# The output projection of a Hymba layer as seven block products, with the sums of its left operands made one product ahead

## The chip, the cores and the metric

The kernel runs on one core of a Trainium2 chip. The metric is the device time of one execution in microseconds (us); each version is run three times or more and the median is taken. The tensor engine is called PE (its weight loads PEld), the vector engine DVE, the scalar engine ACT, GpSimd POOL, and SP is the engine that issues most of the transfers.

## The reference, cut to what matters

One decoder layer is computed for a prompt of 1024 tokens (with 16 meta tokens ahead of it, which are dropped at the end) and for 64 sample tokens (8 sequences of 8). The 16 heads of 128 channels are 6 mLSTM heads (A0 to A5), 6 gated delta rule heads (B0 to B5) and 4 HGRN2 heads (C0 to C3).

```python
D_MODEL = 2048; SEQ = 1024; DEC_BATCH = 8; DEC_SEQ = 8; HEAD_DIM = 128; N_META = 16
MIX = 2048            # 16 heads x 128

# each layer:
#   x += W_out( headRMSNorm(concat[mLSTM heads, gated-DeltaNet heads, HGRN2 heads]) * g * silu(z) )
# all q/k/v/gate columns and the gate z come from one combined projection of RMSNorm(x)
# after the layer:
def _rmsnorm(x, w):
    xf = x.astype(jnp.float32)
    y = xf * lax.rsqrt(jnp.mean(xf * xf, axis=-1, keepdims=True) + EPS)
    return (y * w.astype(jnp.float32)).astype(x.dtype)
```

The output projection, which the change is about, multiplies y (1088 tokens x 2048 channels) by `w_out` (2048 x 2048), in float32. The outputs are the normed sums for the prompt and the sample tokens, and the heads' states.

## The kernel before, in words

**Halves.** The prompt is processed in two halves of 512 tokens; the first also has the 64 sample and the 16 meta tokens (592 columns, `halves[0]`, `half.first`). Each half runs the input projection head by head in the order of `ORDER` (C0 B0 A0 B1 A1 C1 B2 A2 B3 A3 C2 B4 A4 B5 A5 C3), and the scan of each head runs in between.

**Float32 by three products.** The matmuls take float32 operands rounded to a shorter form (`F32R`). So every float32 operand is split in a rounded part (hi, a cast on ACT) and the remainder (lo, a subtraction on DVE), and a product is hi x hi + lo x hi + hi x lo: three matmuls. For weights `feed_split` does this, for y `finish` does. The weights come as pieces of 128 x 512: `pieces` lists them in the order of use, `feed_raw` loads them (256 KB on ACT's queue into `wraw`, 5 buffers) up to 7 ahead, `feed_split` makes `whi` and `wlo` (4 buffers each) up to 3 ahead, and `next_piece` hands out the next.

**The weave.** Scans, finishes and other side work are Python generators in the queues of `Weave` ("scan", "fin", "post", "bg"). Between matmuls, `weave.pump` issues the next step of each queue whose due time has been reached, on a clock that `Clock` and `Engine.cost` keep by estimated costs while the program is written. `drain` and `drain_queue` issue the remaining steps of streams or of a queue, with `pump` alone and no matmul of the projections in between: they push the clock forward to the next due time until those streams are done. Behind that, a scheduler that keeps to the dependencies can still move instructions on each engine, so the order on the engines differs somewhat from the order in the code. All recorded operations carry line 137, the helper's; so groups are told apart by tile names.

**The scans near the change.** The last head is C3. Its scan works in levels: POOL makes X from the exponentials Ex and hk or hq, PE multiplies X into pa, and after the last level hkd and hqd (POOL) feed pkh, puh and poh on PE. After each scan, `finish` normalises the head's output, turns it through DRAM (`turn_out`, `turn_in`: `yd` stores and `s` loads), multiplies it by the gate, splits it (ACT casts into `zs`, POOL subtracts, `y<-y,zs`) and stores both parts in `y_dram`. `load_y` brings them back into the tiles of the projection's input. All transfers other than weight pieces are on SP's queue, in order.

**The output stage.** For each column group `cg` (512 columns) all 16 heads k run over the token tiles of a half: 5 tiles in the first half (the sample tile has 2 products, since both of its y parts lie in one left operand), 4 in the second. Each head's piece is used once per unit. After a unit the sums in PSUM (`oacc`) are added to x (`res`, DVE), squared with a sum along the row (`oscr`, ACT) and multiplied by the final norm's weight (`fnw`, POOL); when all four column groups of a half are done, `final_norm` makes the factor `fr` (a `pow` on POOL), scales and stores. The last column group of the second half is run as two units of two tiles.

Of the kernel before, what the change touches and what calls it, by code (L numbers as in the profile page):

```python
# [13 lines left out]
P = 128  # L14
D = 2048
# [130 lines left out]
class Weave:  # L146
    def __init__(self, clock):
        self.clock = clock
        self.queues = {"scan": [], "fin": [], "post": [], "bg": []}
# [37 lines left out]
OUT_UNITS = ([(cg, range(5)) for cg in range(4)], [(cg, range(4)) for cg in range(3)] + [(3, range(2)), (3, range(2, 4))])  # L187
# [3 lines left out]
def hybrid_step(ctx, tc, i, o):  # L191
# [51 lines left out]
    def o_raw(k, cg):  # L243
        raw = wp.tile([P, 512], F32, tag="wraw", name="wraw", bufs=5)
        WDMA(raw, i["w_out"][0, P * k:P * (k + 1), 512 * cg:512 * (cg + 1)])
        return raw

# [95 lines left out]
    for units in OUT_UNITS:  # L343
        for cg, _ in units:
            for k in range(NK):
                pieces.append((o_raw, k, cg))
# [256 lines left out]
    y_dram = [dp.tile([NH, P, w], F32R, name=f"y{w}") for w in (2 * NSAMP + 2 * HALF, 2 * HALF)]  # L603
# [233 lines left out]

    def finish(half, head, outs, ssq, scale, zs):
# [36 lines left out]
        d = y_dram[half.index][head].bitcast(F32)  # L875
        for part, t in enumerate((yhi, ylo)):
            t = t.bitcast(F32)
            at_ = 2 * NSAMP if half.first else 0
            DMA(d[:, at_ + HALF * part:at_ + HALF * (part + 1)], t[:, 0:HALF])
            if half.first:  # L880
                DMA(d[:, NSAMP * part:NSAMP * (part + 1)], t[:, HALF:WS])
# [90 lines left out]
    def mlstm_scan(half, h, kT, qT, vT, tho, zs, nm, em, st):  # L972
# [118 lines left out]
        weave.add("fin", finish(half, h, hxs, ssq, 0.25, zs))  # L1091
# [60 lines left out]
    def gdn_scan(half, h, ck_, cq, cv, zs, Gb, eG, bb, st):  # L1152
# [242 lines left out]
        weave.add("fin", finish(half, HA + h, hxs, ssq, 1.0, zs))  # L1395
# [22 lines left out]
    def hgrn_scan(half, h, kT, lf, qT, vT, zs, st):  # L1418
# [152 lines left out]
        weave.add("fin", finish(half, HA + HB + h, hxs, ssq, 0.25, zs))  # L1571
# [91 lines left out]
    def load_y(half, g):  # L1663
        w = y_dram[half.index].shape[-1]
        yT[half.index][g] = [hp.tile([P, 2, w], F32R, tag=f"h{g}{part}", name=f"y{g}{part}") for part in (0, 1)]
        for q in range(4):
            DMA(yT[half.index][g][q // 2][:, q % 2].bitcast(F32), y_dram[half.index][4 * g + q].bitcast(F32))

    def y_block(half, k, n, part):

        at_ = HALF * part + P * n
        return yT[half.index][k // 4][k % 4 // 2][:, k % 2, at_:at_ + P]

    hB, yT = {}, [{}, {}]
    for half, groups in zip(halves, group_lists):
# [4 lines left out]
        for n, group in enumerate(groups):  # L1680
# [5 lines left out]
            if half.first and n == 6:  # L1686
                weave.add("bg", prep_B())
            after = None
            if n == len(groups) - 1:
# [3 lines left out]
                else:  # L1693
                    after = lambda g: load_y(halves[0], g)
# [12 lines left out]

    ys_flat = o["y_sample"].rearrange("b t d -> (b t) d")
    tags = ["a", "b", "c", "d", "e", "f", "g", "h", "j", "a", "b", "c", "d", "e", "f", "g", "h", "j", "k", "u"]

    def final_norm(toks, some, res, ss, fr, late):
        for n in some:
            cnt = toks[n][1]
            V.tensor_reduce(fr[:cnt, n:n + 1], ss[:cnt, n], op=ALU.add, axis=AX.X)
            V.tensor_scalar(fr[:cnt, 8 + n:9 + n], fr[:cnt, n:n + 1], 1.0 / D, EPS, op0=ALU.mult, op1=ALU.add)
            G.tensor_tensor(fr[:cnt, 16 + n:17 + n], fr[:cnt, 8 + n:9 + n], halfneg[:cnt, 0:1], op=ALU.pow)
        yield
        for n in some:
            _, cnt, _, dst = toks[n]
            for cg in range(4):  # L1720
                t, r = res[n, cg], fr[:cnt, 16 + n:17 + n]
                if cg == 3 and late:
                    V.scalar_tensor_tensor(t[:cnt], t[:cnt], r, fnw[cg][:cnt], op0=ALU.mult, op1=ALU.mult)
# [112 lines left out]
```

## Time and profile before

| | |
|---|---|
| median of 3 runs | 2504.53 us (2497.64, 2504.53, 2504.58) |
| the profiled execution's own time | 2499.9 us |
| its span, from the first to the last instruction | 2498.2 us |
| mean granted clock of PE | 0.991 |
| busy: PE, PEld, DVE, ACT, POOL | 2437.1, 2181.1, 1441.9, 993.4, 548.7 us |
| moved by DMA | 350.81 MB, 140 GB/s over the span |
| output matmuls, written into `oacc` | 1088 with `whi`, 576 with `wlo` |
| weight pieces: `w_in`, `w_out` | 564 and 144 loads of 256 KB |
| POOL: `res<-res,fnw`, `y<-y,zs` | 34 of 1460 ns, 32 of 1441 ns |
| output stage, first to last output matmul | 2097.5 to 2487.1 us |

The table is read from the page and the windows of the profiled execution; the other rows are shown where they are used. A row of a group gives its line (always 137 here), engine, operation, tiles (out<-in), shape and count, then busy us and the mean ns of one, then how long the engine was idle just before them and what ended that.

### The profile page before, as it was taken

What the parts mean: (1) busy time and instruction counts of PE and PEld (TensorE: products, weight loads), DVE (VectorE), ACT (ScalarE), POOL (GpSimd) and SP (SyncE); (2) the same over time, 40 slices, a digit from 0 to 9 for tenths busy, and PEclk for the clock granted to TensorE, in tenths of its full rate; (3) what the DMA queues carried; (4) which work ended last, traced back from release to release, by engine and by line L of the source; (5) the groups of instructions that cost most, each with busy time, mean ns of one, the idle gap of its engine ahead of it and who ended that gap; (6) DMA issues with size and microseconds to landing.
All of it is one profiled execution on the core that took longest, in us unless ns stands there. A gap on an engine that the chain in (4) does not pass through costs nothing.

```text
span 2498.2 us, 43685 instructions
## 1 busy us (share of the span) xinstructions
PE 2437.1 (98%) x16032; PEld 2181.1 (87%) x16032; DVE 1441.9 (58%) x3080; ACT 993.4 (40%) x2428; POOL 548.7 (22%) x743
## 2 busy tenths in 40 slices
PE   6999999999999999999999999999999999999998
PEld 5999999999999999998787888888888888888886
DVE  7765766766647656556854556554654646333435
ACT  5643444443435334343642343343533334222324
POOL 5331211421204212113320113110310102111201
PEclk9999999999999999999999999999999999999999
DMA  6445756766645445348445445454544559526735
GB/s 138 111 119 144 175 131 135 187 147 159 147 108 142 99 119 146 93 112 244 112 121 123 112 120 135 118 134 98 144 118 112 132 124 307 135 84 201 252 100 181
DMA packets 681043, 350.81 MB, mean 140 GB/s; under 512 B 260004, under 2 KB 622076, under 8 KB 680828
## 3 DMA queue, kind: packets, MB, share of 16 engines
q10 hardware_dynamic: 318528, 185.64, 29.4%
q1 hardware_dynamic: 362300, 162.37, 24.9%
q8 instruction: 126, 2.06, 0.3%
q14 instruction: 89, 0.73, 0.1%
HBM read 285.71 MB, written 62.19 MB: 139 GB/s over the span
## 4 chain that ended last, share of the span: by engine, by line
PE 77%; DVE 8%; DMA 6%; issue 3%; ACT 2%; POOL 2%; SPq 1%; ACTq 0%; DVEq 0%; POOLq 0%
PE acc L137 53%; PE oacc L137 13%; DVE wlo L137 2%; DMA wraw<-in_w_in_dram 2%; PE pa L137 1%; PE po L137 1%; SPq L1209 1%; PE pyy L137 1%; PE nd L137 1%; DMA Bb<-db 1%; ACT whi L137 1%; PE pu L137 1%; PE pz L137 1%; DVE Yc L137 1%; DVE Yt L137 1%
## 5 line engine op out<-in xcount | busy, mean ns | idle before, releaser
L137 DVE TENSOR_TENSOR wlo<-wraw,whi 128x512 fp32r<-128x512 f32 x720 | 540.2, 752 | 552.5 <-ACT whi L137 534.7
L137 PE MATMUL acc<-hA,whi 128*128 128x288 f32 (+1 forms) x4544 | 819.6, 302 | 5.3 <-DVE whi L137 5.1
L137 ACT CAST whi<-wraw 128x512 fp32r<-128x512 f32 x720 | 443.9, 618 | 934.9 <-PE acc L137 427.5
L137 PE MATMUL acc<-hB,whi 128*128 128x512 f32 x2272 | 725.3, 401 | 3.6 <-DMA hB<-hblo 3.1
L137 PEld LDWEIGHTS acc<-hA,whi 128*128 128x128 f32 x4544 | 676.1, 190 | 10.2 <-issue 6.5
L137 PE MATMUL acc<-hA,wlo 128*128 128x288 f32 x2240 | 488.5, 298 | 4.7 <-DVE wlo L137 4.7
L137 PEld LDWEIGHTS acc<-hB,whi 128*128 128x128 f32 x2272 | 415.4, 190 | 85.6 <-DMA hB<-hblo 3.9
L137 PE MATMUL acc<-hB,wlo 128*128 128x512 f32 x1120 | 441.6, 394 | 1.5 <-DVE wlo L137 1.5
L137 PEld LDWEIGHTS acc<-hA,wlo 128*128 128x128 f32 x2240 | 365.7, 189 | 6.3 <-DVE wlo L137 6.3
L137 PE MATMUL oacc<-whi,y 128*128 128x512 f32 x1088 | 343.2, 390 | 0.0
L137 PEld LDWEIGHTS acc<-hB,wlo 128*128 128x128 f32 x1120 | 212.1, 189 | 49.4 <-DVE wlo L137 3.4
L137 PEld LDWEIGHTS oacc<-whi,y 128*128 128x128 f32 x1088 | 204.3, 188 | 42.8 <-ACT whi L137 0.8
L137 PE MATMUL oacc<-wlo,y 128*128 128x512 f32 x576 | 224.6, 390 | 2.0 <-DVE wlo L137 2.0
L137 PEld LDWEIGHTS oacc<-wlo,y 128*128 128x128 f32 x576 | 108.2, 188 | 25.4 <-DVE wlo L137 3.3
L137 POOL TENSOR_TENSOR res<-res,fnw 128x512 f32<-128x512 f32 (+1 forms) x34 | 48.6, 1460 | 258.5 <-ACT oscr L137 258.5
L137 POOL TENSOR_TENSOR y<-y,zs 128x592 fp32r<-128x592 f32 (+1 forms) x32 | 46.1, 1441 | 153.2 <-ACT zs L137 138.9
L137 POOL TENSOR_TENSOR qd<-qT,emb 128x512 f32<-128x512 f32 x12 | 16.9, 1404 | 219.1 <-PE po L137 219.0
L137 DVE TENSOR_TENSOR Yt<-Yc,Bb 128x60 f32<-128x60 f32 (+8 forms) x180 | 36.5, 203 | 47.5 <-DMA Bb<-db 42.4
L137 POOL TENSOR_TENSOR hr<-hr,halfneg 128x4 f32<-128x4 f32 (+1 forms) x48 | 44.7, 931 | 70.3 <-DVE hr L137 69.3
L137 POOL TENSOR_TENSOR nrm<-nrm,halfneg 128x10 f32<-128x10 f32 x12 | 24.0, 1998 | 125.0 <-DVE nrm L137 125.0
L137 POOL TENSOR_TENSOR X<-Ex,hk 128x256 f32<-128x256 f32 (+1 forms) x40 | 39.7, 992 | 52.4 <-PE pa L137 40.7
L137 DVE TENSOR_TENSOR Sx<-Sx,lf 128x256 f32<-128x256 f32 (+2 forms) x60 | 35.3, 590 | 20.8 <-ACT Ex L137 18.9
(416 smaller groups left out, 2748.4 us busy)
## 6 DMA issues: line engine op xcount, KB each, us to landing
wraw<-in_w_in_dram ACTq DMA_DIRECT2D x564, 256.0 KB
wraw<-in_w_out_dram ACTq DMA_DIRECT2D x144, 256.0 KB
y<-y SPq DMA_DIRECT2D x16, 576.0 KB
px<-in_x_prompt_dram SPq DMA_DIRECT2D x32, 256.0 KB
yd<-y SPq DMA_DIRECT2D x128, 64.0 KB
out_dram<-sst SPq DMA_DIRECT2D x16, 512.0 KB
s<-yd SPq DMA_DIRECT2D x32, 256.0 KB
y<-zs SPq DMA_DIRECT2D x32, 256.0 KB
```

Source lines behind the costliest of these rows:

```text
L137: return f(out, *a, **k)
L1209: DMA(db[j], Ball[SUB * j:SUB * (j + 1), 0:C, SUB * j:SUB * (j + 1)])
```

## The change

It replaces the two loops over the prompt's tokens in the output stage by Strassen's scheme with seven products, in Winograd's form. The tokens are split in two halves of 512 (rows of A), the heads in `K1` (the first eight of `ORDER`) and `K2` (the last eight), the columns in groups 0, 1 and 2, 3. A11 is then the first half's y of `K1`, A12 that of `K2`, A21 and A22 those of the second half, and B11, B12, B21, B22 the four blocks of `w_out` (B's rows are heads, its columns `cg`). Each product is 512 tokens x 8 heads x 1024 columns, in two column groups j of 8 heads (kk) and 4 tiles with three matmuls. In the order of the code:

| product | left operand | weights | column groups j = 0, 1 |
|---|---|---|---|
| 1 | A11 | B11 | own pieces of `w_out`; sums kept in `t1` |
| 2 | A12 | B21 | own pieces; added to `res` of the first half's cg 0, 1 |
| 3 | A21 - A11 + A22 | T2 | added to `t1` |
| 4 | A21 + A22 | T1 | with `t1` into `q` |
| 5 | A12 minus the left operand of product 3 | B22 | added to `res` of the first half's cg 2, 3 |
| 6 | A11 - A21 | T3 | into `q` and `t1`, which become the second half's `res` |
| 7 | A22 | T4 | added to the second half's cg 0, 1 |

- **Weights.** `combine_weights` is a new generator in a new queue "mix", started with `prep_B` and working after it: 16 pieces, each with 4 loads of 256 KB from `w_out` into `px`/`pxs`, 4 subtractions on POOL, and 4 stores to `w_comb` in DRAM, loads and stores on SP. Products 3, 4, 6 and 7 load their pieces from there (`c_raw`). The pieces loaded in the output stage are 80 of `w_out` and 72 of `w_comb`, against 144 before.
- **Left operands.** `y_whole` holds plain y in DRAM. In the second half `finish` stores only it: the cast into `zs`, the POOL subtraction and the stores of the two parts are gone, and so is `load_y` of the second half. In the first half `finish` stores plain y beside the parts. `fill` runs as a side job of a product: it loads the blocks of y (`yb`) of the next product's left operand, head by head, sums them on POOL (in one place DVE and POOL), and splits the sum into the idle one of the two sets of left operands (`yT[u]`, alternately 0 and 1): 40 casts on ACT and 40 subtractions on DVE in all.
- **Sample tokens** are still multiplied plainly, beside the products (`own` with the product's piece, `other` with a piece of `w_out` loaded for them): 128 matmuls as before.
- **Sums.** `x_rows` and `x_added` load x and add it on POOL; additions of `oacc` to `t1`, `q` and `res` are on DVE. After product 1's first column group the sums are copied on ACT into `px`/`pxs` tiles, and for that "mix" is drained there. The units of the last product, `LAST_UNITS`, are column group 0 with 4 tiles and column group 1 with 2 and 2 tiles.

The diff, cut to its core:

```diff
+HEADS = [{"A": 0, "B": HA, "C": HA + HB}[name[0]] + int(name[1]) for name in ORDER[1:]]
+K1, K2 = HEADS[:NH // 2], HEADS[NH // 2:]
+LAST_UNITS = [(0, range(4)), (1, range(2)), (1, range(2, 4))]
...
+        if not half.first:
+            DMA(y_whole[1][head], y[:, 0:HALF])
+            return
         yhi, ylo = zs.bitcast(F32R), y.bitcast(F32R)
         S.copy(yhi[:, 0:W], y[:, 0:W])
+        ck.last += 1.0
+        yield
+        DMA(y_whole[0][head], y[:, 0:HALF])
+        ck.last = ck.t["T"] + 2.0
...
+    def combine_weights():
+        while not prep_stream.done:
+            yield
+        for j in range(2):
+            for kk in range(NK // 2):
...
+                for t, heads, cg in ((b11, K1, j), (b12, K1, j + 2), (b22, K2, j + 2), (b21, K2, j)):
+                    tc.keep_in_program_order(DMA(t, i["w_out"][0, P * heads[kk]:P * (heads[kk] + 1), 512 * cg:512 * (cg + 1)]))
+                for dst, a, b in ((b11, b12, b11), (b12, b22, b12), (b22, b22, b11), (b21, b21, b22)):
+                    ck.last = ck.t["T"] + 9.0
+                    yield
+                    G.tensor_tensor(dst, a, b, op=ALU.subtract)
+                ck.last = ck.t["T"] + 20.0
+                yield
+                for n, t in (("T1", b11), ("T3", b12), ("T2", b22), ("T4", b21)):
+                    DMA(w_comb[n][NK // 2 * j + kk], t)
...
+    def phase(u, j, accs, tiles, own=None, other=None, each=()):
+        for kk in range(NK // 2):
+            whi, wlo = next_piece()
+            for n in tiles:
+                yh, yl = (y_block(u, kk, n, part) for part in (0, 1))
+                T.matmul(accs[n], yh, whi, start=kk == 0, stop=False)
+                T.matmul(accs[n], yh, wlo, start=False, stop=False)
+                T.matmul(accs[n], yl, whi, start=False, stop=kk == NK // 2 - 1)
+                if n == tiles[0]:
+                    feed_ahead()
+                weave.pump()
...
+            for g in filling:
+                next(g, None)
+            for f in each:
+                f(NK // 2 * j + kk)
...
+    for j in range(2):
+        accs, sacc = banks(), bank("oacc")
+        phase(0, j, accs, halfn, own=(sacc, samples(0)))
+        if j == 0:
+            weave.drain_queue("mix")
+            ck.begin()
+            for n in halfn:
+                t1[j, n] = sp.tile([P, 512], F32, tag="px" if n < 3 else "pxs", name="t1", bufs=3 if n < 3 else 1)
+                S.copy(t1[j, n], accs[n])
+            held = sacc
+    weave.drain_queue("scan")
+    weave.drain_queue("post")
...
+    fill_with(0, [(1, K1), (1, K2), (0, K1)], [(V, 2, ALU.subtract), (G, 1, ALU.add)])
+    for j in range(2):
+        accs, sacc = banks(), bank("oacc")
+        phase(1, j, accs, halfn, own=(sacc, samples(1)), each=[x_rows(1, 0, t1)])
...
+    fill_with(0, [(1, K2)], [])
+    for j in range(2):
+        accs = banks()
+        phase(1, j, accs, halfn, each=[more(1), x_added(q, 5, 2, 2), x_added(t1, 5, 0, 3)])
```

The order of the instructions on PE at the end of C3's scan, early in the output stage, first as it stands before. X_24193 and X_24221 are the operands of the scan's last two levels, y a left operand of the projection; a wait names the engine or transfer it is for.

```order
L137 MATMUL pa<-X_24193 128x128 x3
L137 MATMUL pa<-X_24221 32x32 [waits Pool_49]
L137 MATMUL pa<-Ex 32x64 x2
L137 MATMUL oacc<-whi,y_23848 128x512 [waits DMAHW2_49,Activation_49]
L137 MATMUL oacc<-wlo,y_23848 128x512 [waits DVE_49]
L137 MATMUL oacc<-whi,y_23925 128x512 [waits DMAHW0_49,Activation_49]
L137 MATMUL pkh<-ident,hkd 128x128 [waits Pool_49]
L137 MATMUL puh<-s_24304,s_24342 128x128 [waits DMAHW6_49,Activation_49]
L137 MATMUL oacc<-whi,y_23925 128x512 [waits DMAHW3_49]
L137 MATMUL poh<-state_C_761,hqd 128x128 [waits DVE_49,Pool_49]
```

These are rows out of a stretch of 50; output matmuls without waits lie between all of the steps. The same place after, where the levels' X are X_24415 and X_24425:

```order
L137 MATMUL oacc<-wlo,y_23982 128x512
L137 MATMUL pa<-X_24415 128x128 [waits DVE_49,Pool_49]
L137 MATMUL pa<-X_24415 128x128 x3
L137 MATMUL pa<-X_24425 32x32 [waits Pool_49]
L137 MATMUL pa<-Ex 32x64 x2
L137 MATMUL pkh<-ident,hkd 128x128 [waits DVE_49,Pool_49]
L137 MATMUL pkh<-ident,hkd 128x128 x3
L137 MATMUL puh<-s_24469,s_24477 128x128 [waits DMAHW3_49,Activation_49]
L137 MATMUL poh<-state_C_767,hqd 128x128 [waits Pool_49]
L137 MATMUL poh<-s_24469,AT 128x128 [waits DVE_49]
L137 MATMUL oacc<-whi,y_23853 128x512
```

From the first pa on X_24415 to the first two matmuls of poh, no output matmul is issued; the rows left out only repeat the kinds of matmul shown. POOL at this place, before:

```order
L137 TENSOR_TENSOR X_24221<-Ex,hk 128x8x32 [waits PE_49]
L137 TENSOR_TENSOR X_24221<-Ex,hq 128x8x32
L137 TENSOR_TENSOR hkd<-Sx,hk 128x512 [waits PE_49,Activation_49]
L137 TENSOR_TENSOR hqd<-eP,hq 128x512 [waits PE_49,Activation_49]
L137 COPY state_C_761<-s_24350 128x128 [waits DVE_49,PE_49]
```

And after, where t is a copy of product 1's sums and yb a block of y for a fill:

```order
L137 TENSOR_TENSOR X_24425<-Ex,hq 128x8x32
L137 TENSOR_TENSOR hkd<-Sx,hk 128x512 [waits PE_49,Activation_49]
L137 TENSOR_TENSOR res<-res,t_24532 128x512 [waits DMAHW0_49,Activation_49]
L137 TENSOR_TENSOR res<-res,t_24534 128x512 [waits DMAHW7_49,DVE_49,Activation_49]
L137 TENSOR_TENSOR res<-res,t_24536 128x512 [waits DMAHW1_49,Activation_49]
L137 TENSOR_TENSOR yb<-yb 128x512 [waits DVE_49]
L137 TENSOR_TENSOR hqd<-eP,hq 128x512 [waits PE_49]
L137 TENSOR_TENSOR res<-res,t_24538 128x512 [waits DMAHW2_49,Activation_49,Pool_49]
```

Three additions of x to product 1's sums and one of a fill now stand between hkd and hqd.

More of the change, by code (lines that the diff above doesn't have):

```diff
@@ L1686, in hybrid_step @@
             if half.first and n == 6:
-                weave.add("bg", prep_B())
+                prep_stream = weave.add("bg", prep_B())
+                weave.add("mix", combine_weights())
             after = None
@@ L1729, in final_norm @@
                 yield
+            free.extend(res.pop((n, cg)) for cg in order)
     def norm_states():
@@ new lines, in hybrid_step @@
+    both = sp.tile([P, 2, 512], F32, tag="sst", name="yb", bufs=1)
+    beside = [[both[:, 0], both[:, 1]], [sp.tile([P, 512], F32, tag=f"vx{n}", name="yb", bufs=1) for n in range(2)],
+              [row("a", "yb")[:, 0:512] for _ in range(2)]]
+    ck.begin()
+    for n in halfn:
+        t1[1, n] = free.pop(0)
+        S.copy(t1[1, n], accs[n])
+    for c in range(4):
+        res[0, c] = free.pop(0)
+    for c in range(2):
+        for at_, cg in ((0, c + 2), (NSAMP, c)):
+            DMA(res[0, c + 2][at_:at_ + NSAMP], xs_flat[:, 512 * cg:512 * (cg + 1)])
@@ new lines, in hybrid_step, with more, f @@
+    weave.add("post", sample_done(0, 1))
+    weave.drain_queue("fin")
+    for tag in "ej":
+        free += [row(tag, "res")[:, 0:512] for _ in range(2)]
+    free += [sp.tile([P, 512], F32, tag=f"s{t}", name="res", bufs=1) for t in "56"]
+    def more(x):
+        def f(step):
+            if step == 2:
+                free.extend(beside[x])
+        return f
+    fill_with(1, [(1, K1), (1, K2)], [(G, 1, ALU.add)])
+    for j in range(2):
+        accs, sacc = banks(), bank("oacc")
+        phase(0, j, accs, halfn, other=(sacc, samples(1)), each=[more(2)])
+        ck.begin()
+        for n in halfn:
+            V.tensor_tensor(t1[j, n], t1[j, n], accs[n], op=ALU.add)
+        sample_add(j + 2, sacc)
@@ new lines, in hybrid_step @@
+    weave.drain_queue("post")
+    load_fnw(2)
+    fill_with(0, [(0, K2)], [(G, "hi", ALU.subtract), (G, "lo", ALU.subtract)])
+    for j in range(2):
+        accs, sacc = banks(), bank("oacc")
+        phase(1, j, accs, halfn, other=(sacc, samples(0)))
+        ck.begin()
+        for n in halfn:
+            q[j, n] = free.pop(0)
+            V.tensor_tensor(q[j, n], t1[j, n], accs[n], op=ALU.add)
+        sample_add(j + 2, sacc)
+        weave.add("post", sample_done(j + 2))
+    weave.add("post", final_norm([0], range(4)))
@@ L1801, in hybrid_step @@
+    load_fnw(0)
+    for j, tiles in LAST_UNITS:
+        accs = banks(tiles)
+        phase(0, j, accs, tiles)
+        weave.drain_queue("post")
+        late = tiles[-1] == NC - 1 and j == 1
+        ck.begin()
+        for n in tiles:
+            t = res[n + 5, j] = t1[j, n]
+            V.tensor_tensor(t, t, accs[n], op=ALU.add)
+            squared(n + 5, j, late)
+        if j == 1:
+            weave.add("post", final_norm([n + 5 for n in tiles], (2, 3, 0, 1), late))
     weave.drain_queue("bg")
```

288 lines of the change are left out of this document (195 added, 93 removed).

## The prediction, before the changed kernel was run

> **What bounds the kernel now.** I read the first lines of the page, then the chain of waits over the last 450 us, then a table of windows through the output stage and two of the projection. The page says that one engine is nearly always at work:
>
> ```profile
> span 2498.2 us, 43685 instructions
> ...
> PE 2437.1 (98%) x16032; PEld 2181.1 (87%) x16032; DVE 1441.9 (58%) x3080; ACT 993.4 (40%) x2428; POOL 548.7 (22%) x743
> ```
>
> The chain shows the same from near: early in the output stage (which starts at 2097.5) it runs along PE, and the end of the scan of the last head (C3: pa, pkh, puh, poh) stands between stretches of output matmuls.
>
> ```profile
> 2126.12 0.89 PE pa L137 x8
> 2127.01 9.55 PE oacc L137 x42
> 2136.56 1.71 PE pa L137 x34
> 2138.26 4.53 PE oacc L137 x19
> 2143.24 1.39 PE oacc L137 x6
> 2144.62 0.91 PE puh L137 x8
> 2145.54 1.86 PE oacc L137 x8
> 2147.39 1.78 PE poh L137 x16
> ...
> 2158.26 149.21 PE oacc L137 x658
> ```
>
> The last row gives the price of one output matmul: 149.21 / 658 = 0.2268 us. The windows (start:end, length, then busy time and count of PE, PEld, DVE, ACT, POOL, then clock, DMA share, GB/s) show how little else the stage costs:
>
> ```profile
> 2158.30:2307.50 149.20, 149.20 (x659) 123.54 (x658) 46.56 (x63) 39.76 (x79) 22.35 (x16) 1.00 0.46 139
> 2307.50:2352.00 44.50, 44.27 (x194) 36.04 (x193) 21.58 (x45) 15.02 (x30) 11.43 (x10) 1.00 0.88 296
> 2352.00:2462.60 110.60, 110.60 (x489) 91.55 (x489) 48.05 (x62) 39.00 (x75) 17.00 (x12) 1.00 0.44 125
> 2462.60:2487.10 24.50, 22.75 (x98) 17.94 (x97) 15.06 (x27) 10.33 (x20) 4.25 (x4) 1.00 0.63 201
> 2487.10:2498.20 11.10, 0.62 (x3) 0.19 (x1) 4.87 (x12) 2.85 (x6) 1.54 (x2) 0.76 0.52 189
> ```
>
> PE loses 0.23 us where the halves meet and 1.75 us near the end; then a tail of 11.1 us follows. So a matmul taken out of this stage is time taken out of the span, as long as its feeders keep up.
>
> **What comes off.** Before, the output stage has 64 + 64 pairs of head and column group: 4 groups x 16 heads x (4 tiles x 3 products + 2 of the sample tile) = 896 in the first half and 768 in the second, 1664. After: seven products x 2 column groups x 8 heads x 4 tiles x 3 = 1344, and the sample's 128 as before, 1472. That is 192 fewer: 192 x 0.2268 = 43.5 us off, the gross gain. PE has no other change: the scans and the projection issue what they issued.
>
> **What is added on the path: the drain of the mix queue.** In the order above the drain after the first column group issues all that C3's scan still has, back to back. Before, by the chain, 42 + 19 + 6 + 8 = 75 output matmuls lie between the pa row at 2126.12 and poh: 9.55 + 4.53 + 1.39 + 1.86 = 17.3 us that cover the work of ACT, POOL and DVE between the levels. This cover goes, but those engines do not begin at the drain: X and the exponentials have been issued ahead. What remains behind the drain on POOL is, by the order, X for the last level, hkd, three additions of t onto res, one yb, and then hqd, which the first poh waits for.
>
> ```profile
> L137 POOL TENSOR_TENSOR hkd<-Sx,hk 128x512 f32<-128x512 f32 x1 | 1.5, 1515 | 2.2 <-PE pa L137 2.2
> L137 POOL TENSOR_TENSOR hqd<-eP,hq 128x512 f32<-128x512 f32 x1 | 1.5, 1495 | 2.6 <-PE pa L137 2.6
> L137 POOL TENSOR_TENSOR res<-res,fnw 128x512 f32<-128x512 f32 (+1 forms) x34 | 48.6, 1460 | 258.5 <-ACT oscr L137 258.5
> ```
>
> These are 1.5 + 3 x 1.46 + 1.46 + 1.5 = 8.8 us on POOL from the last level on, while PE has that level's pa (1.71), puh (0.91) and pkh (no longer than puh): 8.8 - 3.5 = 5.3 us of waiting. The lower bound is 2 us (POOL finishes the additions before the level ends, and only ACT's copies of pkh are waited for), the upper the whole cover, 17 us. I take 5.3, since most of the head's X work is hoisted.
>
> A stop of this length can cost clock as well. Two windows in which PE was idle by about as much:
>
> ```profile
> 1160.00:1170.00 10.00, 7.87 (x43) 6.48 (x41) 5.91 (x14) 3.34 (x8) 2.94 (x4) 1.00 0.81 247
> 1170.00:1180.00 10.00, 8.58 (x35) 6.70 (x36) 4.59 (x8) 2.41 (x5) 1.74 (x2) 0.83 1.16 311
> 1320.00:1330.00 10.00, 7.58 (x96) 5.58 (x95) 5.34 (x19) 1.27 (x3) 1.18 (x3) 0.83 0.38 96
> ```
>
> A mean of 0.83 over 10 us is 1.7 us of lost work; I leave it in the bounds, since the first window kept 1.00 with 2.1 us idle. [...]
>
> **What is added beside the path, projection stage.** The weight combinations are 16 pieces of 4 loads (256 KB), 4 POOL subtractions and 4 stores, from 673 us on: 64 x 1.46 = 93 us more on POOL, less 16 x 1.44 = 23 us (the table's mean) of y<-y,zs that the second half no longer does. POOL has room, and so has DMA:
>
> ```profile
> 300.00:650.00 350.00, 347.08 (x2874) 340.46 (x2872) 232.65 (x537) 146.24 (x398) 86.78 (x124) 1.00 0.67 156
> 700.00:1040.00 340.00, 337.62 (x2799) 330.78 (x2798) 205.82 (x485) 135.77 (x375) 82.71 (x118) 1.00 0.48 119
> ...
> 1040.00:1500.00 460.00, 448.20 (x2842) 386.67 (x2841) 270.98 (x593) 189.03 (x440) 93.15 (x108) 0.99 0.52 133
> 1500.00:2053.00 553.00, 551.48 (x3114) 456.68 (x3113) 305.86 (x644) 208.99 (x497) 100.27 (x112) 0.99 0.50 123
> ```
>
> The first window has the nearest thing to the new stream, the preparation of the second half (`prep_B`, which loads x and stores its two parts through SP; DMA share 0.67): PE idle 2.92 of 350 us. The second has none: 2.38 of 340. So such a stream costs about 0.5 us in 350. The new one is four times as long, and its stores wait on POOL with the scans' transfers behind them on SP; the planner also sets the scans by other costs. I take 2.5 us, with bounds from -3 (the second half's finishes lose their cast, subtraction and stores of the parts; the last window has 1.5 us of idle PE to give and the third might give as much) to +12 (the third window, in which the halves meet, has 11.8 us of idle PE: as much again).
>
> **Output stage, beside the path.** Five fills cast 40 blocks on ACT, subtract 40 + 8 on DVE and do 40 operations on POOL; POOL also adds 32 tiles of x or of a product's sum to it, and multiplies 34 by fnw: 106 operations. With rows:
>
> ```profile
> L137 DVE TENSOR_TENSOR wlo<-wraw,whi 128x512 fp32r<-128x512 f32 x142 | 112.8, 799 | 200.0 <-ACT whi L137 192.5 <-DMA wraw<-in_w_out_dram 7.4
> L137 ACT CAST whi<-wraw 128x512 fp32r<-128x512 f32 x141 | 87.4, 621 | 235.8 <-PE oacc L137 173.3 <-DVE wlo L137 20.7 <-DMA wraw<-in_w_out_dram 12.2
> L137 DVE TENSOR_TENSOR res<-res,oacc 128x512 f32<-128x512 f32 (+1 forms) x36 | 23.0, 677 | 10.4 <-PE oacc L137 10.3
> ...
> L137 DVE TENSOR_SCALAR res<-res,fr 128x512 f32<-128x512 f32 (+1 forms) x25 | 13.0, 555 | 5.4 <-POOL fr L137 5.4
> L137 POOL TENSOR_TENSOR fr<-fr,halfneg 128x1 f32<-128x1 f32 (+1 forms) x9 | 7.6, 863 | 21.6 <-DVE fr L137 21.6
> ```
>
> DVE: 152 wlo x 0.80 + 48 x 0.80 + 72 additions x 0.68 + 25 x 0.56 = 223 us. ACT: (152 + 40) x 0.62 = 119, beside as many squares as before. POOL: 106 x 1.46 = 155. PE: 1472 x 0.2268 = 333.8. No engine is near PE on average. The tightest places: the third and fourth products need two pieces per 14 matmuls (3.18 us) where DVE gives 2 x 0.80; the last unit uses one piece per 6 matmuls (1.36 us), as before, and loses what it loses now, the 1.52 us here:
>
> ```profile
> 2470.51 0.50 PE L137 MATMUL oacc<-wlo,y 128*128 128x512 f32 x1 [1.52 <-DVE wlo L137]
> ```
>
> In the sixth product DVE's scalings by fr wait for POOL's pow, with wlo queued behind them; POOL's own queue has the x additions ahead of pow. One POOL operation more in front is 1.46 us, and three pieces stand ready (3 x 12 x 0.2268 = 8.2 us), so I put 2 us on it, from 0 to 8. The last unit now has 8 heads instead of 16: its pieces still come at the same rate, 0.5 us more. The tail has the same operations and stores as now: nothing.
>
> **Sum.** -43.5 + 5.3 + 2.5 + 2 + 0.5 = -33.2 us. Against the profiled execution (2499.9 us, span 2498.2) this is 2466.7. The median of the runs, 2504.53, stands 4.6 us above that execution, the lowest run 2.3 below; I forecast 2468 us for a run like the profiled one, which leaves 1.3 us for that spread.
>
> **Rivals.** (a) The drain loses the whole cover, 17 us, and a clock window, 1.7: 2468 + 11.7 + 1.7 = about 2481. For it: the order leaves one output matmul in the whole stretch. Against it: ACT's and POOL's part of the levels is issued earlier.
>
> (b) DVE becomes the bound of the output stage through POOL. For it: beside POOL's work single wlo take far longer, as here, where POOL's X runs:
>
> ```profile
> 2106.02 1.35 DVE L137 TENSOR_TENSOR wlo<-wraw,whi 128x512 fp32r<-128x512 f32 x1
> ```
>
> From 2158 to 2487 most take half of that (min/median/max in ns):
>
> ```profile
> L137 DVE TENSOR_TENSOR wlo<-wraw,whi x125: 673/693/1843, 2160.6 to 2483.6; 128x512 fp32r<-128x512 f32 x125
> ```
>
> If every POOL operation stops DVE for all its 1.46 us, DVE needs 152 x 0.69 + 48 x 0.69 + 72 x 0.68 + 25 x 0.56 + 155 = 356 us against 334 of PE: 22 us more, 2490. Against it: the mean wlo of the stage is 0.80 and not 0.69 with 34 multiplications on POOL, 142 x 0.11 = 16 us in all and not 34 x 1.46 = 50, and PE lost 1.98 us in the windows above. [...]
>
> (c) The other side: SP is held by the combination's stores. Each piece keeps SP waiting for POOL up to 4 x 1.46 = 5.8 us, 16 pieces 93 us; the scans' transfers queue behind, and heads come late to PE. It decides when more than 33 us of the 93 reach PE beyond the 2.5 of the sum; with half of the 93 the time is 2468 + 46 = 2514. Against it: 1.5 us of idle PE in the 553 us of the last window of the projection, so PE has projection matmuls to do beside scans that come late.
>
> (d) Fewer matmuls without less time, since pieces or y blocks arrive late: the change then only moves the wait to the loads. The window with DMA share 0.88 moved 296 GB/s and cost PE 0.23 us. Of the products after, the third needs up to 16 pieces + 16 blocks of 256 KB (0.262 MB) in the 25.4 us of a column group (112 x 0.2268), 330 GB/s; the sixth some 30 transfers in 21.8 us, 360 GB/s. At 296 GB/s each column group of the third ends 2.9 us late and each of the sixth 4.8, in two and two 15.4 us: 2483. Against it: a fourth of the sixth's are stores, which no matmul waits for. To cancel the change all fourteen column groups would have to be late by 2.4 us.
>
> **Chances.** Forecast 0.65 (its own range 2457 to 2478), (a) 0.12, (d) 0.07, (b) 0.05, (c) 0.07, and 0.04 for an end below 2456, by better covered scans. The range from 2456 to 2489 takes in the forecast, (a) and (d), and leaves out the rest. A difference below 0.3%, 7.5 us, can't be told from none: faster is below 2497, which holds everything but (c): 0.93. (c) has same, 0.02, where little more than a third of its 93 us reaches PE, and slower, 0.05.
>
> **What the next profile would show.** 192 fewer oacc matmuls at 0.227 us. One gap or several short ones on PE, about 5 us, between pa and poh some 25 us into the output stage, with POOL's hqd as the releaser; 17 us would be (a). PE idle in 673 to 2097 as now within some us; if it grows by tens, with SP waiting on POOL, (c). In the output stage a mean wlo near 0.85 us; above 1.2 with PE waiting for wlo throughout, (b). Waits of whi for wraw in the third and fourth products, (d). The forecast is wrong most easily at the drain, and where the order of the scans in the projection stage is moved by the planner's new costs.

## The result, and the profile after

The changed kernel is slower: 2534.23 us in the median of 4 runs (2526.65 to 2546.85) against 2502.68 in the runs of the kernel before that were made beside it; the ratio is 1.0134, with a 95% interval from 1.0088 to 1.0180. The forecast was 2468. The profiled execution took 2537.37 us, its span is 2535.7 us, 37.5 more than before. First the page:

```profile
span 2535.7 us, 44051 instructions
...
PE 2422.4 (96%) x15840; PEld 2160.8 (85%) x15840; DVE 1550.4 (61%) x3168; ACT 1018.6 (40%) x2476; POOL 715.8 (28%) x865
```

192 matmuls are gone, as counted, but PE's busy time fell by 14.7 us only and not by 43.5, and its share fell from 98% to 96%. A table of windows shows where; the first window is the projection, the second the output stage. Before:

```profile
0.00:2097.40 2097.40, 2048.75 (x14267) 1860.42 (x14268) 1272.16 (x2820) 863.34 (x2172) 474.93 (x682) 0.99 0.55 135
2097.40:2487.20 389.80, 387.82 (x1766) 320.54 (x1765) 164.99 (x250) 127.26 (x252) 72.25 (x59) 1.00 0.55 168
```

And after:

```profile
0.00:2132.80 2132.80, 2060.40 (x14266) 1869.22 (x14267) 1298.28 (x2821) 857.27 (x2158) 535.99 (x731) 0.98 0.59 149
2132.80:2524.80 392.00, 361.89 (x1576) 291.62 (x1574) 247.75 (x337) 158.47 (x312) 178.29 (x132) 0.96 0.63 195
```

Both parts failed. The projection, with the same number of matmuls, ends 35.4 us later: PE idles 23.7 us more (72.4 against 48.65) and is busy 11.65 us longer, at a clock of 0.98. The output stage takes 2.2 us more instead of 43.5 less: 28.1 us more idle (30.1 against 2.0), and its 190 fewer matmuls save 25.9 us of busy time instead of 43.5, at a clock of 0.96. The tail is unchanged (10.9 us). What PE waits for in the output stage (us in total, times, longest):

```profile
PE oacc L137 <- ACT whi L137: 14.1, 4, 7.3
PE oacc L137 <- DVE wlo L137: 13.3, 13, 2.5
PE puh L137 <- ACT s L137: 1.6, 1, 1.6
```

So the split weights come late. The longest wait can be followed through the engines' timelines. On SP (L1818 loads x, L1901 a block of y for a fill):

```profile
2387.77 27.36 SPq L1818 DMA_DIRECT2D yb<-in_x_prompt_dram  x9
2415.18 8.08 SPq L1901 DMA_DIRECT2D yb<-yw  x4
```

On ACT, the first cast after that, and the weight cast behind it:

```profile
2419.17 0.62 ACT L137 CAST y<-yb 128x512 fp32r<-128x512 f32 x1 [14.09 <-DMA yb<-yw]
2419.69 0.61 ACT L137 CAST whi<-wraw 128x512 fp32r<-128x512 f32 x1
```

And on PE:

```profile
2420.36 0.79 PE L137 MATMUL oacc<-whi,y 128*128 128x512 f32 x1 [7.34 <-ACT whi L137]
```

Nine loads of x stood on SP for 27 us. The issue of one took 0.33 us in seven of the nine, 0.60 and 0.66 in the other two; for most of the rest SP waited, 12.5 us for POOL's additions, which free the buffers, and 10.0 us for earlier loads of x. The next blocks of y stood behind them on SP, ACT stood 14.1 us for such a block, and the weight cast stood behind that on ACT, although its weights were there (by 2413.4 us). The wait costs more than its length, since the granted clock falls around it:

```profile
2410.00:2420.00 10.00, 3.02 (x9) 2.01 (x7) 0.18 (x1) 0.83 (x2) 7.25 (x6) 0.67 0.42 141
2420.00:2430.00 10.00, 9.62 (x30) 7.35 (x31) 5.57 (x9) 4.87 (x9) 0.00 (x0) 0.70 0.61 192
2430.00:2440.00 10.00, 10.00 (x46) 8.29 (x45) 9.51 (x21) 6.00 (x14) 7.84 (x7) 1.00 0.36 116
```

In the second of these windows PE is busy for 9.62 us and finishes 30 matmuls instead of 42 (9.62 / 0.2268): 2.8 us more than 30 need.

### The profile page after: what moved, and what is told of

It is laid out like the page before. It is cut to its first block, busy times and chain, and to the rows that moved or that the text cites. A ratio compares the mean times of both kernels' runs of the same rounds, so it can differ in the third digit from the quotient of the medians.

```text
span 2535.7 us, 44051 instructions
## 1 busy us (share of the span) xinstructions
PE 2422.4 (96%) x15840; PEld 2160.8 (85%) x15840; DVE 1550.4 (61%) x3168; ACT 1018.6 (40%) x2476; POOL 715.8 (28%) x865
## 4 chain that ended last, share of the span: by engine, by line
PE 62%; DVE 12%; DMA 11%; issue 4%; POOL 4%; ACT 3%; SPq 3%; ACTq 1%; DVEq 0%; POOLq 0%
PE acc L137 47%; PE oacc L137 5%; DVE wlo L137 4%; DMA wraw<-in_w_in_dram 2%; DMA yb<-yw 2%; SPq L1247 2%; DMA Bb<-db 2%; ACT whi L137 1%; PE po L137 1%; PE pyy L137 1%; PE nd L137 1%; DVE Yt L137 1%; POOL yb L137 1%; DVE Yc L137 1%; POOL res L137 1%
## 5 line engine op out<-in xcount | busy, mean ns | idle before, releaser
L137 DVE TENSOR_TENSOR wlo<-wraw,whi 128x512 fp32r<-128x512 f32 x728 | 572.8, 791 | 444.4 <-ACT whi L137 424.8
L137 PE MATMUL oacc<-whi,y 128*128 128x512 f32 x960 | 312.2, 400 | 15.0 <-ACT whi L137 14.1
L137 PEld LDWEIGHTS oacc<-whi,y 128*128 128x128 f32 x960 | 185.5, 193 | 56.3 <-ACT whi L137 16.3
L137 PE MATMUL oacc<-wlo,y 128*128 128x512 f32 x512 | 205.8, 402 | 13.5 <-DVE wlo L137 13.3
L137 PEld LDWEIGHTS oacc<-wlo,y 128*128 128x128 f32 x512 | 98.9, 193 | 41.1 <-DVE wlo L137 20.8
L137 DVE TENSOR_TENSOR y<-yb,y 128x512 fp32r<-128x512 f32 x40 | 36.7, 918 | 47.5 <-ACT y L137 46.7
L137 ACT CAST y<-yb 128x512 fp32r<-128x512 f32 x40 | 24.8, 620 | 82.4 <-POOL yb L137 38.7
L137 POOL TENSOR_TENSOR res<-res,fnw 128x512 f32<-128x512 f32 (+1 forms) x28 | 41.8, 1510 | 42.3 <-ACT oscr L137 42.3
L137 POOL TENSOR_TENSOR yb<-yb 128x512 f32<-128x512 f32 x24 | 34.3, 1432 | 60.3 <-DMA yb<-yw 42.6
```

The costliest lines, as they stand in the source:

```text
L137: return f(out, *a, **k)
```

## The experiments

Two readings serve for all runs: where the projection ends and how long the output stage is, in each run's profiled execution, since the whole time mixes both. Their repeatability follows from kernels that leave one part as it is. With the projection of the changed kernel it ended at 2122.0 to 2137.2 us in eight profiles; with its output stage, that stage took 383.5 to 396.5 in nine. So about 8 us either way can't be told. Ratios are to the kernel before.

### The output stage: the fills

**e1_no_fill**

```diff
     def fill_with(*a):
-        filling.append(fill(*a))
+        pass
```

> All five fills are left out (no blocks of y loaded, summed, cast or split in the output stage), so products 3 to 7 multiply whatever the two sets of left operands held before; matmuls, weight pieces, x rows, squares and stores stay. The output stage took 392.0 us in the changed kernel (2132.8 to 2524.8) where 1472 matmuls at 0.2268 and the scan would be 346. Theory W: the fills' casts on ACT and subtractions on DVE wait for POOL and SP, and weight casts queue behind them: the stage falls to 350-362, PE's waits there from 29.9 us to under 8. Rival L (POOL and DVE lock each other, whoever issues): POOL keeps 66 of its 106 operations, so the stage stays above 372. Rival S (the rest of the side work, x rows and the sample's sums, waits as much): also above 372. Projection as in the changed kernel, 2133 within 8.

```profile
2132.60:2485.70 353.10, 347.07 (x1576) 286.78 (x1574) 196.33 (x289) 138.25 (x272) 123.03 (x92) 0.99 0.55 166
```

353.1 us and 6.0 idle, at 2494.8 us in all (ratio 0.9968, 0.9955 to 0.9982). The forecast for this stage was 389.8 - 43.5 + 5.3 + 2 + 0.5 = 354: without the fills the gain is there, and the fills take 39 us, all of it. The x rows, squares and sums that stay are not the cause by themselves.

**e2_fill_no_wait**

```diff
+                still = yT[1 - u][(kk - 2) // 2][:, (kk - 2) % 2, 2 * NSAMP:2 * NSAMP + HALF].bitcast(F32)
-                S.copy(hi, beside[0][kk % 2])
+                S.copy(hi, still)
...
-                V.tensor_tensor(lo, beside[0][kk % 2], hi, op=ALU.subtract)
+                V.tensor_tensor(lo, still, hi, op=ALU.subtract)
```

> The fills keep every instruction (loads, sums, 40 casts, 40 subtractions), but the casts and subtractions read a block that has long been ready (the hi part of the other set of left operands) instead of the sum; so nothing on ACT or DVE waits for a fill's load or POOL sum, at the same busy time of every engine. Theory W: output stage 392 to 355-370, and waits of PE for whi and wlo from 27 us to under 12. Rival L (the lock, or sheer work): still above 382.

```profile
2131.20:2530.60 399.40, 360.18 (x1576) 292.53 (x1574) 244.74 (x339) 159.50 (x314) 182.22 (x132) 0.95 0.63 195
```

399.4 us, ratio 1.0156 (1.0127 to 1.0186): no gain. But the edit does less than was expected of it. The first fill has eight sums on DVE, and these still wait for its loads, 17.2 us against 4.7 in the changed kernel. And ACT's weight casts now wait for transfers of blocks of y, though they read none:

```profile
DVE yb L137 <- DMA yb<-yw: 17.2, 7, 5.3
ACT whi L137 <- DMA yb<-yw: 15.1, 3, 6.4
ACT whi L137 <- DMA yb<-in_x_prompt_dram: 9.2, 3, 6.2
```

PE's waits for whi and wlo fell from 27.4 to 16.2 us, and the one of 7.3 us is gone. In its place stand two others:

```profile
PE puh L137 <- ACT s L137: 9.5, 1, 9.5
PE oacc L137 <- DVE res L137: 8.7, 2, 7.1
```

The first comes from the DVE sums: DVE's copy of product 1's sample sums stands behind three of them, and ACT's copy s behind that. So e2 neither shows theory W nor refutes it. The loads of the weights are issued on ACT's queue, ahead of the casts, and in the order of e2's program 77 of the stage's 152 wait for one of the eight DMA semaphores that both queues use. That this links the casts to the blocks of y is inferred; no run took it away.

**e5_no_fill_loads, e6_no_fill_sums**: one half of the chain each.

```diff
 # e5
-                    DMA(beside[x][kk % 2], y_whole[half][heads[kk]])
+                    pass
 # e6
-                    e.tensor_tensor(srcs[0], srcs[0], srcs[b], op=op)
-                    ck.sync()
+                ck.sync()
```

> The fills' 72 loads of y blocks are left out (the blocks hold one block loaded once); the sums on POOL and DVE, the casts and the subtractions stay, in their order and with their waits on each other. Theory Q (the transfers: SP's loads wait for buffers that POOL releases late, ACT's casts and the weight loads issued on ACT's queue wait for them, and the 8 DMA semaphores are shared by both queues): the output stage falls from 392 to 354-368. Rival P (the work on POOL and the lock between POOL and DVE): it stays above 380. If both are one chain, this and the next fall.

> The fills' sums (40 operations on POOL, 8 on DVE) are left out; the 72 loads, 40 casts and 40 subtractions stay, so another left operand is multiplied. Rival P: the output stage falls from 392 to 354-368. Theory Q with transfers slow by themselves: above 380. If the loads are slow only because POOL releases their buffers late, it falls here as well as without the loads.

Without the loads, then without the sums:

```profile
2137.20:2497.80 360.60, 349.73 (x1576) 284.94 (x1574) 260.39 (x337) 159.50 (x312) 191.49 (x132) 1.00 0.54 167
```

```profile
2122.00:2492.70 370.70, 354.67 (x1576) 291.10 (x1574) 229.03 (x331) 159.47 (x313) 123.23 (x92) 0.97 0.66 208
```

360.6 and 370.7 of 392.0 (ratios 1.0011, 0.9996 to 1.0025, and 1.0032, 1.0016 to 1.0048): taking away either half brings back 31 and 21 us of the 39. Above the 353.1 us without fills, the sums alone cost 7.5 us and the loads alone 17.6, of which the wait of puh has 5.6 (6.8 us against 1.2); both together cost 39. So the greater part of the loss comes from the two as one chain. e6 ended 3 us above its range. The first row also refutes the lock of rivals L and P, DVE stopped by POOL, as the cause: all of POOL's sums are there, a wlo is as long as in the changed kernel (0.93 us against 0.90), and the stage is 31 us shorter. The wlo groups without loads, without sums:

```profile
L137 DVE TENSOR_TENSOR wlo<-wraw,whi 128x512 fp32r<-128x512 f32 x160 | 146.2, 929 | 72.4 <-ACT whi L137 71.8
```

```profile
L137 DVE TENSOR_TENSOR wlo<-wraw,whi 128x512 fp32r<-128x512 f32 x155 | 126.2, 829 | 89.1 <-ACT whi L137 87.5 <-DMA wraw<-T 1.1
```

With POOL's sums a wlo took 0.10 us longer (0.929 against 0.829, and 0.830 in e1, which has neither), 16 us of DVE in all. PE feels little of it: in e5 it waits 9.1 us for wlo in all, and never more than 1.8.

What SP waits for in the changed kernel's stage shows the chain's other end (L1901 the blocks of y, L1818 x):

```profile
SPq L1901 <- DVE y L137: 87.6, 27, 11.7
SPq L1901 <- POOL yb L137: 46.4, 20, 5.5
```

A block's buffer comes free when POOL has summed it, ACT has cast it and DVE has made the remainder; SP stands until then with the following transfers behind it.

**e9_fill_loads_pool, e12_both**: the loads on another queue; e12 also has the combinations on DVE (e10, below).

```diff
-                    DMA(beside[x][kk % 2], y_whole[half][heads[kk]])
+                    nc.gpsimd.dma_start(beside[x][kk % 2], y_whole[half][heads[kk]])
```

> The fills' 72 loads of y blocks are issued on POOL's queue instead of SP's; nothing else changes. Theory Q (with the loads on SP each waits there for a buffer that POOL, ACT and DVE release one after another, and the x rows and weights wait with them): the output stage falls from 392 to 360-375. Rival: the loads now wait in POOL's own queue, ahead of its sums, and the stage is no shorter than 385.

> Loads of the fills on POOL's queue and combinations on DVE together, everything computed as in the changed kernel. If both help by themselves the two add: projection 2108-2120, output stage 360-375, about 2490; otherwise the sum of the two single results within 8 us.

The stage took 415.1 and 411.6 us, with waits of PE for one weight cast up to 12.9 us; ratios 1.0221 (1.0194 to 1.0249) and 1.0201 (1.0184 to 1.0218). The waiting moved into POOL's own queue, where the loads (L1901) now stand for a buffer, in e9:

```profile
POOL yb L1901 <- DVE y L137: 32.9, 15, 13.9
```

**e14_fill_in_order, e17_deeper**: order and depth.

```diff
 # e14: sums, casts and subtractions of the fills
-                S.copy(hi, beside[0][kk % 2])
+                tc.keep_in_program_order(S.copy(hi, beside[0][kk % 2]))
 # e17: four buffers in products 2 to 4
+    extra = [free.pop(0) for _ in range(4)]
+    deeper += [extra[:2], extra[2:]]
...
+                ahead = len(bufs[x]) - 2
+                for n in (range(ahead + 1) if kk == 0 else [kk + ahead]):
```

> The fills' sums, casts and subtractions may not be moved ahead of anything written before them on their engine. If the order in the queues makes the waits: the output stage falls from 392 to 360-375. If the chain load, sum, cast, subtraction, next load is too long for two buffers whatever the order: 385 or more.

> Everything computed as in the changed kernel, with three edits: the blocks of y of the fills in products 2, 3 and 4 have four buffers instead of two and are loaded two blocks sooner (in product 2 two of the three operands); the first half's finish stores plain y without the shifted steps; the weight combinations' subtractions are on DVE. Projection: 2096.9 without combinations and shifts, some 13 us more with the combinations on DVE, 2105-2115. Output stage: if two buffers were too few, PE's waits in products 3 to 5 go and the stage is 370-380 of 392 (products 6 and 7 keep theirs); if the transfers or the work are slow by themselves, 387 or more. Time 2488-2500 in the first case, 2505-2515 in the second.

390.8 and 392.6 us: neither the order on the engines nor the number of buffers alone changes the stage. In e17 8.4 us of it are the wait of puh (1.6 in the changed kernel), so up to 7 us may be hidden; but PE's waits of over 0.5 us between 100 and 260 us of the stage, where products 3 to 5 lie, still add up to 10.7 us, against 11.5 in the changed kernel. e17 took 2522.67 us (1.0076, 1.0049 to 1.0102), above the time expected, yet the fastest of the kernels that compute everything, through its projection (2107.9). It still has a wait of 7.2 us in product 6, which it did not touch.

**e18_no_added_loads**: the 16 loads of x in product 6, those seen above among them.

```diff
-                pend.append((dst[j, n], x_load(n + n0, j + cg0)))
+                pend.append((dst[j, n], free.pop(0)))
```

> The 16 loads of x in product 6 are left out (POOL adds what the buffers hold); POOL's additions, and the loads of the blocks of y behind them on SP, stay. If SP's order is the cause there: the wait of 7.3 us for a weight cast goes, with its lowered clock, and the output stage is 374-384 instead of 392. If not (the wait comes from POOL's work or ACT's own order): 388 or more.

```profile
PE oacc L137 <- DVE wlo L137: 17.5, 12, 3.0
PE puh L137 <- ACT s L137: 4.2, 1, 4.2
PE oacc L137 <- ACT whi L137: 2.0, 2, 1.1
```

The waits for weight casts fell from 14.1 to 2.0 us and the one of 7.3 is gone: that wait comes from the loads of x on SP. (The edit takes away the loads themselves, not only their place in the queue.) It is no accident of one run: with the same output stage it stands at the same place, 7.5 us long, in e3 and e7. The stage took 384.9 us, 7 less than in the changed kernel, just above the range expected and within the spread; the rest of the loss sits in many waits of 1 to 3 us for wlo.

### The projection: combinations and the finish

**e3_no_mix, e7_mix_no_pool, e8_mix_no_dma**: without the combinations, then with their transfers alone, then with their POOL work alone.

```diff
 # e3; products 3, 4, 6, 7 load plain pieces
-                weave.add("mix", combine_weights())
 # e7
-                    G.tensor_tensor(dst, a, b, op=ALU.subtract)
+                    ck.begin()
 # e8: four tiles loaded once; plain pieces
-                    DMA(w_comb[n][NK // 2 * j + kk], t)
```

> The weight combinations are left out (no loads, POOL subtractions and stores beside the projection); products 3, 4, 6 and 7 load plain pieces of w_out of the same size instead. The projection ended at 2132.8 us against 2097.4 before, 35.4 later: 23.7 of waiting of PE and 11.7 of longer matmuls at a lower clock. Theory M (the mix stream on POOL and SP delays the scans): the projection ends at 2100-2112 and the time falls by 20 us or more. Rival F (the first half's finish, with its extra store and shifted steps, or the order that follows from it): the end stays above 2120; the lag of 6 us at 260 us of the span, ahead of the stream, stays in both.

> The weight combinations' 64 POOL subtractions are left out; the 64 loads and 64 stores stay, so plain blocks of w_out are multiplied. The whole stream cost the projection 23 us (end at 2132.8 with it, 2109.9 without). If POOL's work ahead of the scans' is what costs: the end falls to 2115 or sooner. If SP's queue and DMA: it stays above 2123.

> The weight combinations' loads and stores are left out and their 64 POOL subtractions stay, on four tiles that are loaded once; the products load plain pieces of w_out. If POOL's work costs: the projection ends above 2123. If SP's queue and DMA: at 2115 or sooner.

The projection ended at 2109.7, 2110.3 and 2161.6 us (ratios 1.0050, 1.0034 to 1.0065; 1.0037, 1.0020 to 1.0053; 1.0224, 1.0201 to 1.0247). The first two:

```profile
0.00:2109.70 2109.70, 2055.44 (x14265) 1867.79 (x14266) 1272.16 (x2820) 857.92 (x2158) 446.45 (x667) 0.99 0.54 135
0.00:2110.30 2110.30, 2053.90 (x14266) 1865.75 (x14267) 1274.47 (x2821) 857.69 (x2158) 447.59 (x667) 0.99 0.58 151
```

The stream costs 23 us, and all of it goes with the 64 subtractions on POOL: without them its 128 transfers of 256 KB beside the projection cost nothing that shows. That does not say in which queue the loss arises, since e7 also ends SP's waiting for the subtractions. In the changed kernel the stores (L1728) stand for POOL 64.3 us in all, with the scans' transfers behind them on SP:

```profile
SPq L1728 <- POOL px L137: 48.9, 28, 5.5
SPq L1728 <- POOL pxs L137: 15.4, 12, 2.8
```

That is rival (c) of the prediction, and no run takes it away by itself. In e8 nothing holds the subtractions back, and they stand in a row, which shows what POOL's queue alone can cost, with no stores on SP:

```profile
700.00:800.00 100.00, 82.93 (x679) 79.80 (x677) 47.45 (x94) 24.28 (x63) 77.92 (x65) 0.91 0.36 90
```

POOL is busy for 78 of 100 us, the scans' operations wait behind it, and PE, which had no idle time in these 100 us before, loses 17 us and clock (0.91).

**e10_mix_dve, e13_mix_in_order**: the same subtractions on DVE; or on POOL, but not moved ahead of what was written before them.

```diff
 # e10
-                    G.tensor_tensor(dst, a, b, op=ALU.subtract)
+                    V.tensor_tensor(dst, a, b, op=ALU.subtract)
 # e13
-                    G.tensor_tensor(dst, a, b, op=ALU.subtract)
+                    tc.keep_in_program_order(G.tensor_tensor(dst, a, b, op=ALU.subtract))
```

> The weight combinations' 64 subtractions are made on DVE instead of POOL (0.69 us each by the output stage's rows instead of 1.46); loads and stores stay. If it is POOL's queue, in which the scans' operations stand behind them, the projection ends at 2108-2120 instead of 2132.8. If any engine of the scans is as bad a place (DVE is 61% busy against 28%): 2130 or later.

> The weight combinations' POOL subtractions may not be moved ahead of anything written before them on POOL; everything is computed as in the changed kernel. If waiting at the head of POOL's queue for a load is the cause: POOL's 108 us of waiting for px fall below 30 and the projection ends at 2108-2118 instead of 2132.8. If it is the 93 us of work: above 2126.

2123.2 and 2137.9 us. DVE's gain of 9.6 is at the edge of the spread and between the two ranges expected; 13 of the 23 us remain there, with SP's stores waiting for DVE. In e13 POOL's waiting for a piece's loads fell, first the changed kernel, then e13:

```profile
POOL px L137 <- DMA px<-in_w_out_dram: 108.4, 13, 21.6
```

```profile
POOL px L137 <- DMA px<-in_w_out_dram: 36.4, 5, 13.0
```

and the end did not move forward. But SP's waiting for POOL grew at the same time, from 64.3 to 132.2 us:

```profile
SPq L1728 <- POOL px L137: 88.7, 34, 8.0
SPq L1728 <- POOL pxs L137: 43.5, 11, 11.8
```

So whether the work in POOL's queue, POOL's waiting there or SP's waiting for POOL delays the scans is not decided by these runs.

**e4_old_finish, e11_no_mix_old_finish, e16_no_mix_no_shift**: the first half's finish.

```diff
 # e4, e11: both edits out; e16: only the shifts out
-        ck.last += 1.0
-        yield
-        DMA(y_whole[0][head], y[:, 0:HALF])
-        ck.last = ck.t["T"] + 2.0
```

> The first half's finish is that of the kernel before (no plain store of y, no shifted steps); the fills load second-half blocks where they loaded first-half ones, so their sums are other numbers at the same cost. Rival F: the lag of about 6 us at 260 us of the span goes and the projection ends 8 us or more sooner than 2132.8. Theory M: the end moves by less than 5.

> No weight combinations and the first half's finish of the kernel before; what is left of the change ahead of the output stage is the second half's shorter finish and the order that the planner makes of it. The projection ended 12.5 us later than before without the combinations alone, and 4.4 us sooner than in the changed kernel with the old finish alone. If these two are all: it ends within 4 us of 2101. If the second half's order costs as well: above 2106.

> No weight combinations (plain pieces of w_out instead) and the first half's finish with its plain store but without the shifted steps. Without combinations the projection ended at 2109.9 with store and shifts, at 2092.6 with neither. If the store costs (POOL's next subtraction waits for its end): above 2105. If the shifted steps do: below 2098.

2128.2, 2092.4 and 2096.7 us. With the combinations the old finish moves the end by 4.6, within the spread. Without them the three steps are 2109.7 (store and shifts), 2096.7 (store) and 2092.4 (neither): the shifted steps cost 13 us, the store 4 at most. So 2092.4 is 5 us sooner than before, and sooner than the 2097 to 2105 expected, which the second half's shorter finish may have earned. e11 and e16 ran at 0.9974 (0.9956 to 0.9993) and 0.9978 (0.9963 to 0.9993) of before without making the combinations, with the slow output stage.

**e15_all_in_order**: e13, e14, and the finish's subtraction later and in order.

```diff
-        ck.last = ck.t["T"] + 2.0
+        ck.last = ck.t["T"] + 6.0
         yield
-        G.tensor_tensor(ylo[:, 0:W], y[:, 0:W], yhi[:, 0:W], op=ALU.subtract)
+        tc.keep_in_program_order(G.tensor_tensor(ylo[:, 0:W], y[:, 0:W], yhi[:, 0:W], op=ALU.subtract))
```

> Both of the above, and the first half's finish has its POOL subtraction 6 us of the planner's clock behind the plain store instead of 2, also in order. If all waiting at queue heads is the cause: projection at 2095-2110, output stage 360-375, a time near 2480, faster than before. If it is work: within 8 us of 2534.

2117.5 us, a stage of 397.2, ratio 1.0107 (1.0079 to 1.0136): the ranges for waiting at queue heads are missed, and the time, 2531.17 us, is the one expected for work; but SP's waiting for POOL is as large here as in e13 (145 us), so this does not decide between the queues either. The end is 4.5 us before the earliest of the eight above, too little to be told.

## Why the prediction was wrong

**What comes off** was right: 192 matmuls, and without the fills the stage is 36.7 us shorter (353.1 against 389.8), where its terms add up to 35.7. That this is so near is in part luck: in e1 PE's busy time fell by 40.75 us and not by 43.5, and the wait at the drain was 1.2 us and not 5.3.

**The drain** was oversized. The term was 5.3 us with bounds of 2 and 17; the wait is 1.6 us:

```profile
2162.14 0.48 PE oacc L137 x2
...
2164.58 0.69 DVE res L137
2165.29 0.58 ACT oscr L137
2165.89 0.60 ACT s L137
2166.53 1.16 PE puh L137 x8
...
2168.38 1.36 PE poh L137 x12
```

The chain leads over DVE's and ACT's copies of product 1's sample sums to the copy that puh needs, and not over POOL's three additions to hqd. In the eighteen other runs the wait of puh was 0.7 to 9.5 us, below 2 in nine and above 4 in eight (4.2 in e18, 9.5 in e2), each time for that copy on ACT. So 5.3 was within what occurs, and the named releaser was not the one.

**The projection's term** was mis-sized: 2.5 us, from -3 to 12; it measured 35.4. Two things failed in it. The nearest row was taken for the stream's transfers (the preparation of the second half), and they cost nothing, as e7 shows; the 93 us of POOL work were set against POOL's mean share and called room. In e8, where these subtractions stand in a row, they cost 52 us (2161.6 against 2109.7), so the mean share does not price them; in the changed kernel they and the waiting for them cost 23. And the shifted steps of the first half's finish were not costed at all: "the planner also sets the scans by other costs" was all that was said of them, and they cost 13 us alone. Rival (c) saw a loss in this stream, on SP; it is not refuted, since SP did stand 64.3 us for POOL there while PE's idle time from 673 us on grew from 15.7 to 31.6, and only transfers that waited for no subtraction were free. The two causes do not add: 23 for the combinations with the shifts, 36 without (2128.2 - 2092.4).

**The output stage's term** failed most: 2 us, from 0 to 8; the fills cost 39. The reading that no engine's busy time bounds the stage was right (DVE 223 us expected and 248 of 392 measured), and it decides nothing here. The step that failed is that only one wait with something queued behind it was looked for (DVE behind pow in product 6). The fills put waits for a transfer and for POOL into the queues of ACT, DVE and SP, in front of the weights' split, and a reserve of three pieces, 8.2 us, did not cover a stop of 14.1 us on ACT.

**Rivals.** (b), DVE stopped by POOL, is refuted as the cause by e5; a wlo took 0.93 us there, with POOL's sums beside it, and 0.83 in e6, without them. (d), blocks that arrive late, was the right kind and the wrong reason: it asked for GB/s, and the blocks were late because their loads stood in SP's queue (195 GB/s over the stage, 296 had been seen). (a) did not happen.

**The clock** was left in the bounds of the drain alone. PE was busy 17.6 us longer in the stage than the count says (43.5 - 25.9); I put this down to the clock, of which a mean of 0.96 over 362 us gives about 14. In the projection it was 11.65 us. There the 20 us around a wait of 6.5 us that ended at 227 us had a clock of 0.74 (0.83 before), and those around one of 2.2 us at 868 had 0.91. The windows around the wait of 7.3 us had 0.67, 0.70, then 1.00; behind the wait of 2.2 us it was 0.50 from 870 to 872 us. In e5, whose longest wait is 1.8 us, the stage kept 1.00. From what length on a wait lowers the clock is not shown.

**What stays open.** Whether POOL's subtractions make PE late through POOL's queue or through SP's waiting for them, and at which operation of the scans; why the shifted steps cost 13 us; whether the semaphores that both queues share carry the waits in e2; and the 31 us by which the stage of e18 stands above the 354 of the forecast, for which no single link was found: order and depth alone changed nothing, and the other queue made it worse. No version that computes everything beat the kernel before: the best, e17, stood 0.8% above it.

## What to carry to other kernels

When work is moved beside a full engine, follow every new wait along the queue in which it stands: what stands behind it, and how long the reserve of the bound engine lasts; the sums of busy time and of GB/s said nothing on that here (DVE busy 248 of 392 us, 195 GB/s). A helper engine with a mean share of 22%, as POOL had before, need not be free: 64 operations more, with the waiting for them, cost 23 us here. Price a second user of it by the time that it holds the queue, four operations of 1.3 to 1.6 us in a row here (740.4 to 746.5 us), and by the other queues that wait for its results. And a long stop of the full engine can cost more than its length, here 2.8 us of slower matmuls behind a wait of 7.3, while the ten waits for wlo in e5, 9.1 us together, left the clock at 1.00.

## What the runs showed of the hardware

Waits of PE of up to 1.8 us, eleven of them in 361 us (e5), left the granted clock at 1.00; around one of 7.3 us two windows of 10 us had 0.67 and 0.70. Loads issued on POOL's queue (e9) made the stage 23 us longer than the same loads on SP's. And 128 transfers of 256 KB more beside the projection (e7: 154 GB/s instead of 130 from 673 us on) cost PE nothing that could be measured, where none of them waited for a subtraction.
